# Longer DMA rows, products on one engine, and a dealing of tokens in two groups, in a scale-and-duplicate kernel

## The chip, the cores and the metric

The kernel runs on 1 core of one Trainium2 chip. The time is the device time of one execution in microseconds, of which several are taken; the figure for a kernel is the median of its runs. A profile is one execution taken by the hardware profiler. Its span runs from the first to the last instruction of the program; the execution's own time is a little longer.

## The reference

Each of 16 x 1024 = 16384 tokens is a vector of 512 fp32 numbers. It is written out twice (k = 2), each copy multiplied by one weight of its own:

```
batch, seq, hidden = 16, 1024, 512;  k = 2
x_expanded = x[:, :, np.newaxis, :].repeat(k, axis=2)
weights = expert_weights[..., np.newaxis]
return (x_expanded * weights).astype(np.float32)
```

The expert indices are an input and are not used. The program reads 2 KB per token and writes 4 KB: 33.6 MB in, 67.1 MB out, with 32768 products of a 512-vector and a number, done for 128 tokens at a time.

## The kernel before, in words

The tokens are dealt to the 128 SBUF partitions in equal runs: partition p has tokens 128p to 128p + 127. So in DRAM the input of neighbouring partitions lies 256 KB apart, the output 512 KB. All weights are loaded once into `w_tile` (L44).

The loop takes 8 tokens per partition in each of 16 iterations. `issue_load` (L48) takes an input tile from `x_pool` (three buffers of 16 KB per partition) and fills it with two DMAs of 4 tokens each (L53, L54), both issued from ScalarE's queue; a DMA is 1 MB, one row of 8 KB for each partition. Two tiles are asked for ahead of the loop, and each iteration first asks for the tile two ahead. The DMA instruction stands in ScalarE's program between the products, so it is issued when ScalarE gets there and when the buffer is free.

Each iteration has two halves of 4 tokens. A half takes an output tile from `o_pool` (six buffers of 16 KB per partition), makes 8 products, one for each token and each of the two weights, and stores the tile with one DMA of 2 MB from SyncE's queue (L93), a row of 16 KB for each partition. The eight products of the first half are all on ScalarE (L79). In the second half product 0 is on VectorE and product 4 on GpSimd (L85), six on ScalarE. Nothing else orders the work: a store waits for its products, a product for its load and for a free output tile, a load for the products on the tile that it overwrites. The framework adds these waits from the use of the tiles; it also has a fixed number of DMA semaphores that it hands out in turn, so a DMA may also wait for an older DMA that had the same one.

The lines that matter: L44 weights, L53 and L54 loads, L79 ScalarE products, L85 VectorE and GpSimd products, L93 stores.

Of the kernel before, what the change touches and what calls it, by code (L numbers as in the profile page):

```python
# [1 line left out]

# [4 lines left out]


@with_exitstack
def kernel(  # L10
    ctx: ExitStack,
    tc: tile.TileContext,
    x: bass.AP,
    expert_indices: bass.AP,
    expert_weights: bass.AP,
    out: bass.AP,
):
    nc = tc.nc

    batch, seq, hidden = x.shape  # L20
    k = expert_weights.shape[-1]
    P = nc.NUM_PARTITIONS
    ntok = batch * seq
    assert ntok % P == 0
    A_TOTAL = ntok // P

    xr = x.rearrange("b s h -> (b s) h").rearrange("(p a) h -> p a h", a=A_TOTAL)
    outr = out.rearrange("b s k h -> (b s) (k h)").rearrange(
        "(p a) n -> p a n", a=A_TOTAL
    )  # L30
    wr = expert_weights.rearrange("b s k -> (b s) k").rearrange(
        "(p a) k -> p a k", a=A_TOTAL
    )

    A = 8
    H = A // 2
    n_iters = A_TOTAL // A

    w_pool = ctx.enter_context(tc.tile_pool(name="w_pool", bufs=1))
    x_pool = ctx.enter_context(tc.tile_pool(name="x_pool", bufs=3))  # L40
    o_pool = ctx.enter_context(tc.tile_pool(name="o_pool", bufs=6))

    w_tile = w_pool.tile([P, A_TOTAL, k], mybir.dt.float32)
    nc.sync.dma_start(out=w_tile, in_=wr)  # L44

    x_tiles = {}

    def issue_load(j):  # L48
        if j >= n_iters:
            return  # L50
        t = x_pool.tile([P, A, hidden], mybir.dt.float32)
        a0 = j * A
        nc.scalar.dma_start(out=t[:, 0:H, :], in_=xr[:, a0 : a0 + H, :])  # L53
        nc.scalar.dma_start(out=t[:, H:A, :], in_=xr[:, a0 + H : a0 + A, :])  # L54
        x_tiles[j] = t

    issue_load(0)
    issue_load(1)

    for it in range(n_iters):  # L60
        a0 = it * A
        issue_load(it + 2)
        x_tile = x_tiles.pop(it)

        for half in range(2):
            o_tile = o_pool.tile([P, H, k, hidden], mybir.dt.float32)
            base = half * H
            opc = 0
            for ai in range(base, base + H):
                for kk in range(k):  # L70
                    w_ap = w_tile[:, a0 + ai, kk : kk + 1]
                    eng = nc.scalar
                    if half == 1:
                        if opc == 0 or opc == 8:
                            eng = nc.vector
                        elif opc == 4:
                            eng = nc.gpsimd
                    if eng is nc.scalar:
                        nc.scalar.mul(  # L79
                            out=o_tile[:, ai - base, kk, :],  # L80
                            in_=x_tile[:, ai, :],
                            mul=w_ap,
                        )
                    else:
                        eng.tensor_scalar(  # L85
                            out=o_tile[:, ai - base, kk, :],
                            in0=x_tile[:, ai, :],
                            scalar1=w_ap,
                            scalar2=None,
                            op0=mybir.AluOpType.mult,  # L90
                        )
                    opc += 1
            nc.sync.dma_start(  # L93
                out=outr[:, a0 + base : a0 + base + H, :], in_=o_tile
            )


# [1 line left out]
_INS = ['x', 'expert_indices', 'expert_weights']  # L99
_OUTS = [((16, 1024, 2, 512), 'float32')]  # L100


# [23 lines left out]
```

## Time and profile before

| | us |
|---|---|
| median of 4 runs | 243.84 |
| lowest and highest | 242.65 and 247.66 |
| the profiled execution, its own time | 243.26 |
| its span | 241.2 |
| ScalarE busy | 140.2 |
| GpSimd busy | 29.7 |
| VectorE busy | 7.9 |

The page says that 100.82 MB were moved, a mean of 418 GB/s over the span, in 9363 DMA packets; 1040 of them are under 512 bytes (semaphore updates, 16 for each of 65 DMAs). Issues of DMAs by kind, with the count, the KB of each and the median time in us from issue to landing:

```profile
out_dram<-o_tile SPq DMA_DIRECT2D x32, 2048.0 KB, 25.3
t<-in_x_dram ACTq DMA_DIRECT2D x32, 1024.0 KB, 28.1
w_tile<-in_expert_weights_dram SPq DMA_DIRECT2D x1, 128.0 KB, 4.6
```

How to read the lines: a product group names the line, the engine, the operation, the tile written and the tiles read, the shape and the count; after the bar stand the busy time in us and the mean of one in ns, after the second bar the time for which the engine sat idle before these instructions and what ended that. DVE is VectorE, ACT is ScalarE, POOL is GpSimd, SPq and ACTq are the sequencers of SyncE and ScalarE as they issue DMAs. A row of the timeline has the start, the time it took, and what ran. In the picture of 40 slices a digit is the busy share of a slice in tenths, 9 being 90% or more.

### The profile page before, as it was taken

The numbers are of one execution on the slowest core, as the hardware profiler recorded it, in microseconds if no ns is written. First come the engines' busy times: TensorE is split into PE (matmuls) and PEld (weight loads), VectorE is DVE, ScalarE is ACT, GpSimd is POOL, SyncE is SP. The second block draws the span as 40 slices with busy tenths as digits, with TensorE's granted clock in tenths as the row PEclk, the third lists the DMA queues.
The fourth block names the chain that finished last, engine by engine and source line by source line (L and its number), as shares of the span: only waits on it lengthen the run. The fifth ranks groups of instructions, "written<-read, shape, count | busy, mean of one in ns | idle before, by whom it ended". The sixth has DMA issues, their size and how long they took to land.

```text
span 241.2 us, 500 instructions
## 1 busy us (share of the span) xinstructions
DVE 7.9 (3%) x16; ACT 140.2 (58%) x225; POOL 29.7 (12%) x20
## 2 busy tenths in 40 slices
DVE  0000000000000000000000000000000000000000
ACT  1989874909458192773918549095590996563000
POOL 0330303002030110302002030020301103020000
DMA  7999999999999999999999999999999999999994
GB/s 254 427 368 429 424 429 444 421 429 423 428 440 418 439 418 436 432 425 435 421 435 431 427 437 420 433 431 425 442 420 433 429 432 435 420 439 431 424 435 201
DMA packets 9363, 100.82 MB, mean 418 GB/s; under 512 B 1040, under 2 KB 1168, under 8 KB 1168
## 3 DMA queue, kind: packets, MB, share of 16 engines
q1 hardware_dynamic: 4752, 67.24, 65.2%
q10 hardware_dynamic: 4608, 33.56, 33.5%
q14 instruction: 3, 0.02, 0.0%
HBM read 33.69 MB, written 67.11 MB: 418 GB/s over the span
## 4 chain that ended last, share of the span: by engine, by line
DMA 83%; ACT 3%; ACTq 0%; issue 0%
DMA t<-in_x_dram 83%; ACT o_tile L79 3%; ACTq L121 0%; ACTq L79 0%
## 5 line engine op out<-in xcount | busy, mean ns | idle before, releaser
L79 ACT ACTIVATE o_tile<-t,w_tile 128x512 f32<-128x512 f32 x224 | 138.9, 706 | 73.5 <-DMA t<-in_x_dram 71.9
L85 POOL TENSOR_SCALAR o_tile<-t,w_tile 128x512 f32<-128x512 f32 x16 | 29.5, 1842 | 187.4 <-DMA t<-in_x_dram 187.4
L85 DVE TENSOR_SCALAR o_tile<-t,w_tile 128x512 f32<-128x512 f32 x16 | 7.9, 492 | 208.0 <-DMA t<-in_x_dram 208.0
L79 ACT ACT_TABLE_LOAD x1 | 1.3, 1283 | 5.4 <-DMA w_tile<-in_expert_weights_dram 5.4
L110 POOL MEMSET const-float32-0.0<- 128x1 f32 x1 | 0.1, 98 | 0.2 <-issue 0.2
L110 POOL MEMSET const-bfloat16-1.0<- 128x1 bf16 x1 | 0.1, 102 | 0.0
L110 POOL MEMSET const-uint8-127<- 128x1 uint8 x1 | 0.1, 101 | 0.0
L110 POOL MEMSET const-float32-1.0<- 128x1 f32 x1 | 0.1, 98 | 0.0
## 6 DMA issues: line engine op xcount, KB each, us to landing
out_dram<-o_tile SPq DMA_DIRECT2D x32, 2048.0 KB, 25.3
t<-in_x_dram ACTq DMA_DIRECT2D x32, 1024.0 KB, 28.1
w_tile<-in_expert_weights_dram SPq DMA_DIRECT2D x1, 128.0 KB, 4.6
```

Of the source, the lines that this page charges most:

```text
L79: nc.scalar.mul(out=o_tile[:, ai - base, kk, :], in_=x_tile[:, ai, :], mul=w_ap,)
L85: eng.tensor_scalar(out=o_tile[:, ai - base, kk, :], in0=x_tile[:, ai, :], scalar1=w_ap, scalar2=None, op0=mybir.AluOpType.mult,)
L110: nc = _bacc.Bacc("TRN2", target_bir_lowering=False, num_devices=1)
```

## The change

- Tokens are dealt in two groups. The first 65 x 128 tokens are dealt in runs of 65 to each partition, the other 63 x 128 in runs of 63. In DRAM the rows of neighbouring partitions lie 130 KB (input) and 260 KB (output) apart in the first group, 126 and 252 KB in the second.
- Loads are larger: five of 13 tokens in the first group, then 16, 16, 16 and 15 in the second, one DMA for each tile, rows of 26 to 32 KB per partition. There are two input buffers of 32 KB per partition (before: three of 16 KB).
- Stores are of 8 tokens, and of the 5 or 7 that are left over at the end of an input tile: rows of 32, 20 or 28 KB. There are four output buffers of 32 KB per partition (before: six of 16 KB).
- All 256 products are on VectorE. ScalarE's queue only issues loads, SyncE's queue only the two weight loads (one for each group) and the stores. No load is asked for ahead of the loop by hand: the first two go out at once, since there are two free tiles, and each later one when its tile is free.

The core of the diff, old lines with a minus, new ones with a plus:

```
-    A = 8
-    H = A // 2
-    n_iters = A_TOTAL // A
+    TX = 16
+    TO = 8
+    groups = [[[13], [13], [13], [13], [13]], [[16], [16], [16], [15]]]
...
-    x_pool = ctx.enter_context(tc.tile_pool(name="x_pool", bufs=3))
-    o_pool = ctx.enter_context(tc.tile_pool(name="o_pool", bufs=6))
+    x_pool = ctx.enter_context(tc.tile_pool(name="x_pool", bufs=2))
+    o_pool = ctx.enter_context(tc.tile_pool(name="o_pool", bufs=4))
...
+    def rows(of_all, done, T):
+        return of_all[done * P : (done + T) * P, :].rearrange(
+            "(p a) n -> p (a n)", a=T
+        )
...
+    for group in groups:
+        T = sum(sum(t) for t in group)
+        xr = rows(xf, done, T)
+        outr = rows(of, done, T)
+        a0 = 0
+        for pieces in group:
+            x_tile = x_pool.tile([P, TX * hidden], f32)
+            at = 0
+            for n in pieces:
+                nc.scalar.dma_start(
+                    out=x_tile[:, at * hidden : (at + n) * hidden],
+                    in_=xr[:, (a0 + at) * hidden : (a0 + at + n) * hidden],
+                )
+                at += n
+            ends = [sum(pieces[: i + 1]) for i in range(len(pieces))]
+            first = 0
+            for t in range(at):
+                if t % TO == 0:
+                    o_tile = o_pool.tile([P, TO * row], f32)
                 for kk in range(k):
...
-                    eng = nc.scalar
-                    if half == 1:
-                        if opc == 0 or opc == 8:
-                            eng = nc.vector
-                        elif opc == 4:
-                            eng = nc.gpsimd
...
+                    nc.vector.tensor_scalar(
+                        out=o_tile[:, o : o + hidden],
+                        in0=x_tile[:, t * hidden : (t + 1) * hidden],
+                        scalar1=w_tile[:, c : c + 1],
+                        scalar2=None,
+                        op0=mybir.AluOpType.mult,
+                    )
+                if t + 1 in ends or (t + 1) % TO == 0:
+                    nc.sync.dma_start(
+                        out=outr[:, (a0 + first) * row : (a0 + t + 1) * row],
+                        in_=o_tile[:, first % TO * row : (t % TO + 1) * row],
+                    )
+                    first = t + 1
+            a0 += at
+        done += T
```

More of the change, by code (lines that the diff above doesn't have):

```diff
@@ L25 @@
     A_TOTAL = ntok // P
[L27 to L33, printed above, removed]
-    A = 8
-    H = A // 2
-    n_iters = A_TOTAL // A
-    w_pool = ctx.enter_context(tc.tile_pool(name="w_pool", bufs=1))
-    x_pool = ctx.enter_context(tc.tile_pool(name="x_pool", bufs=3))
@@ L41 @@
-    o_pool = ctx.enter_context(tc.tile_pool(name="o_pool", bufs=6))
[L43 to L69, printed above, removed]
-                for kk in range(k):
-                    w_ap = w_tile[:, a0 + ai, kk : kk + 1]
-                    eng = nc.scalar
-                    if half == 1:
-                        if opc == 0 or opc == 8:
-                            eng = nc.vector
-                        elif opc == 4:
-                            eng = nc.gpsimd
[L78 to L95, printed above, removed]
@@ new lines @@
+    f32 = mybir.dt.float32
+    row = k * hidden
+    TX = 16
+    TO = 8
+    groups = [[[13], [13], [13], [13], [13]], [[16], [16], [16], [15]]]
+    assert sum(sum(sum(t) for t in g) for g in groups) == A_TOTAL
+    xf = x.rearrange("b s h -> (b s) h")
+    of = out.rearrange("b s k h -> (b s) (k h)")
+    wf = expert_weights.rearrange("b s k -> (b s) k")
+    w_pool = ctx.enter_context(tc.tile_pool(name="w_pool", bufs=1))
+    x_pool = ctx.enter_context(tc.tile_pool(name="x_pool", bufs=2))
@@ new lines @@
+    o_pool = ctx.enter_context(tc.tile_pool(name="o_pool", bufs=4))
+    w_tile = w_pool.tile([P, A_TOTAL * k], f32)
+    def rows(of_all, done, T):
+        return of_all[done * P : (done + T) * P, :].rearrange(
+            "(p a) n -> p (a n)", a=T
+        )
+    done = 0
+    for group in groups:
+        T = sum(sum(t) for t in group)
+        nc.sync.dma_start(
+            out=w_tile[:, done * k : (done + T) * k], in_=rows(wf, done, T)
+        )
+        done += T
+    done = 0
+    for group in groups:
+        T = sum(sum(t) for t in group)
+        xr = rows(xf, done, T)
[15 more added lines that the diff above has]
+                    o_tile = o_pool.tile([P, TO * row], f32)
+                for kk in range(k):
+                    c = (done + a0 + t) * k + kk
+                    o = t % TO * row + kk * hidden
+                    nc.vector.tensor_scalar(
[6 more added lines that the diff above has]
+                if t + 1 in ends or (t + 1) % TO == 0:
+                    nc.sync.dma_start(
+                        out=outr[:, (a0 + first) * row : (a0 + t + 1) * row],
+                        in_=o_tile[:, first % TO * row : (t % TO + 1) * row],
+                    )
+                    first = t + 1
+            a0 += at
+        done += T
```

## The prediction

> **What bounds the kernel now.** I read the 40 slices and the DMA queues on the page first, because one row there is full from end to end:
>
> ```profile
> DMA  7999999999999999999999999999999999999994
> ...
> q1 hardware_dynamic: 4752, 67.24, 65.2%
> q10 hardware_dynamic: 4608, 33.56, 33.5%
> ```
>
> The two queues (q1: stores and the weights, q10: loads) fill 65.2 + 33.5 = 98.7% of the sixteen DMA engines' span. ScalarE, the busiest compute engine, is at 58%. So the question is what the change does to the bytes per us of the DMA engines and to the stretches where they lack work. The next view is the table of stretches: span, then busy us of VectorE, ScalarE and GpSimd, the clock, the DMA share and GB/s.
>
> ```profile
> 0.00:4.00 4.00, 0.00 (x0) 0.00 (x0) 0.19 (x4) 1.00 0.53 163
> 5.00:13.00 8.00, 0.49 (x1) 7.61 (x12) 1.84 (x1) 1.00 1.01 428
> 14.00:17.00 3.00, 0.00 (x0) 2.37 (x5) 1.32 (x1) 1.00 0.98 289
> 17.00:19.00 2.00, 0.00 (x0) 2.00 (x4) 0.00 (x0) 1.00 1.07 459
> 18.00:218.00 200.00, 6.90 (x14) 127.14 (x206) 25.78 (x14) 1.00 1.01 430
> 220.00:236.00 16.00, 0.00 (x0) 0.00 (x0) 0.00 (x0) 1.00 1.01 432
> 237.00:241.20 4.20, 0.00 (x0) 0.00 (x0) 0.00 (x0) 1.00 0.24 101
> ```
>
> Loads alone (5 to 13 us) move 428 GB/s, stores alone (220 to 236) 432, both together 430. The span splits accordingly: 100.82 MB at 430 GB/s is 234.5 us; the remaining 6.7 us are 2.5 lost in the first 4 us (0.65 MB, 1.5 us' worth), 0.85 lost between 14 and 19 us (1.79 MB in 5 us), and 3.2 lost after 237 us. Nothing else can be won or lost but these.
>
> Third, the groups, for the duration of each kind of product, and the timeline of ScalarE, whose 15 in a row show the distance from one start to the next:
>
> ```profile
> L79 ACT ACTIVATE o_tile<-t,w_tile 128x512 f32<-128x512 f32 x224 | 138.9, 706 | 73.5 <-DMA t<-in_x_dram 71.9
> L85 POOL TENSOR_SCALAR o_tile<-t,w_tile 128x512 f32<-128x512 f32 x16 | 29.5, 1842 | 187.4 <-DMA t<-in_x_dram 187.4
> L85 DVE TENSOR_SCALAR o_tile<-t,w_tile 128x512 f32<-128x512 f32 x16 | 7.9, 492 | 208.0 <-DMA t<-in_x_dram 208.0
> ```
>
> ```profile
> 0.71 0.40 ACTq L53 DMA_DIRECT2D t<-in_x_dram  x1
> ...
> 6.67 9.29 ACT L79 ACTIVATE o_tile<-t,w_tile 128x512 f32<-128x512 f32 x15
> 8.51 0.49 DVE L85 TENSOR_SCALAR o_tile<-t,w_tile 128x512 f32<-128x512 f32 x1 [8.51 <-DMA t<-in_x_dram]
> 8.58 1.84 POOL L85 TENSOR_SCALAR o_tile<-t,w_tile 128x512 f32<-128x512 f32 x1 [8.16 <-DMA t<-in_x_dram]
> 11.71 32.60 SPq L93 DMA_DIRECT2D out_dram<-o_tile  x7
> ```
>
> VectorE's first product starts at 8.51, when tile 0's second half has landed; the first store is issued at 11.71.
>
> **Part 1: longer rows.** A DMA moves one row per partition, so 8 rows per DMA engine. Before, an engine moves 32 x 8 = 256 load rows of 8 KB and 256 store rows of 16 KB; after, 9 x 8 = 72 load rows of 26 to 32 KB and 18 x 8 = 144 store rows of 20 to 32 KB. The bytes are the same. The rates above price a row: 8192 x 16 / 428 GB/s = 306.2 ns for a load row, 16384 x 16 / 432 GB/s = 606.8 ns for a store row; 8 KB more cost 300.6, so 5.6 ns are fixed per row. The trace's packet records say the same (309 and 611 ns at the median, so 302 per 8 KB and 7 fixed). There are 512 - 216 = 296 rows fewer per engine: 296 x 5.6 = **-1.7 us**; ends 0 (the fit does not carry to 32 KB) and -2.1 (7 ns). By the fit a 32 KB row takes 1.208 us, a 26 KB row 0.983, a 20 KB row 0.757.
>
> **Part 2: row pitch (65 and 63 tokens).** The distance between partitions' rows in DRAM goes from 256 and 512 KB to 126 to 260 KB, no power of two. In the packet records store rows take 611 ns at the 5th, 50th and 95th percentile, load rows 309: none waits for a place in memory. I take 0; the price if this is wrong is in the rivals. The Trainium skill ("DMA: Bandwidth & Descriptors", Latency and other measured facts) gives 207 GB/s per direction at a pitch of 512 KiB against 214 once padded, on copies between DRAM tensors, and advises padding. By that ratio the stream here would gain about 3%, an estimate of 7 us; the equal rates of 428 at one pitch and 432 at twice that pitch speak against it.
>
> **Part 3: products to VectorE.** Removed: 224 ScalarE products, its table load, 16 GpSimd products. Added: 240 on VectorE. Its 16 products of before all came after a wait, at 0.49 us each. On ScalarE one takes 0.706 us, but 15 stand in 9.29 us: (9.29 - 0.71) / 14 = 0.61 from start to start, 0.87 of a duration. I take 0.87 x 0.49 = 0.42 us on VectorE, ends 0.39 (0.49 less ScalarE's 0.09) and 0.49. All 256 then take 108 us (125 at most) against some 232 of DMA: hidden in the middle, on the path only at the start. The skill ("VectorE: DVE Perf Modes", the errata section) gives 58 cycles + 512/2 at 0.96 GHz, an estimate of 0.33 us, by which the gap of part 4 would be zero; no row here shows it.
>
> **Part 4: the start.** The first load grows from 1 to 3.4 MB, and only two loads (6.8 MB) can be issued before products free a tile; before it was 6.3 MB in six. Tile 0 of before is 16 rows x 0.306 = 4.9 us and was usable at 8.51, so 3.6 us are start and landing. After: 3.6 + 8 x 0.983 = 11.5, and 11.6 with the second weight DMA (8 short rows per engine). Load 1 ends 7.9 later, less about 0.5 for landing: the loads run dry at **19.0**. Store 0 needs 16 products: 11.6 + 16 x 0.42 = 18.3 (17.8 to 19.4). From issue to first row: the first load, with nothing queued ahead, was issued at 0.71 and its first row stands at 1.92 in the packet records, 1.2 us; the first store, with over 1 MB of loads ahead, was issued at 11.71 and its first row stands at 15.84, 4.1 us. After the change next to nothing is queued ahead, so I take 1.3 and keep 4.1 as the other end. First store row 19.6: DMA idles **+0.6 us**; ends 0 and 4.5 (19.4 + 4.1 - 19.0).
>
> Past that the engines stay fed. Store 1 and load 2 are issued at 18.3 + 10 x 0.42 = 22.5, while store 0 (8 x 1.208 = 9.7 us) runs; store 0, load 2 and store 1 hold 9.7 + 7.9 + 6.1 = 23.7 us of work, to 43; store 2 joins at 29, store 3 and load 3 at 33, another 23.7. In the steady state a token costs VectorE 0.84 us and the DMA engines 128 x 6 KB at 434 GB/s, 1.81 us; while VectorE fills one output tile (6.7 us) up to three others (29 us of rows) are queued. This cover also holds at the end, so the tail stays; if it failed, each store would add its products' 6.7 us.
>
> **Part 5: queues and waits.** ScalarE's queue now holds loads alone, so none stands behind products; each from the third on waits for the last product on its tile, and in the built order some also for an older store to be complete. Behind it are only later loads. On SyncE 18 stores stand behind each other, each waiting for its own products; a late one delays only stores that VectorE makes later anyway. Cost 0, hidden by the same backlog.
>
> **Two unpriced terms.** The 0.85 us dip at 14 to 19 us, where the load rows just ahead of the first stores took about 530 ns instead of 309, may vanish (loads are over by then) or repeat: 0 to -0.85; I take 0. The sixteen engines finished between 237.7 and 239.8 us; with rows twice as long the last may end one old row later, 0 to +0.6; I take 0.
>
> **Sum**, against the profiled execution: 241.2 - 1.7 + 0.6 = 240.1 us of span. That execution took 243.26 us, 2.06 outside the span: 242.2. The median of the runs shown, 243.84, is 0.6 above it, so I forecast **242.7**. Own range: -2.1 and -0.85 without a gap, 240.9; no row saving, a gap of 0.6 and +0.6, 245.0.
>
> **Rivals.** (A) Slower: the first store comes late. Place: DMA idle from 19.0. It decides once the first store row stands after 19.0 + 1.7 = 20.7 us. With 4.1 us from issue to row it is 22.4, a gap of 3.4: 243.84 - 1.7 + 3.4 = 245.5; with 0.49 us per product also, gap 4.5, 246.6. For it: the only store that the trace shows starting. Against it: the queue ahead is empty here.
> (B) Faster by pitch: the equal rates hide a loss common to loads and stores. The best slice of before ran at 444 GB/s; all bytes at that take 227.1 us, 7.4 less: 236.4, and 237.0 with the gap. Against it: constant row times.
> (C) The good ends together: dip gone, gap nil, 2.1 saved: 240.9.
> (D) Rows of 32 KB run slower per byte than the fit, say by the 1% between 428 and 432: 2.3 us lost in place of 1.7 won, with the gap 243.84 + 2.9 = 246.7. No row of this length is in the trace.
>
> **Numbers.** Forecast 0.62, A 0.15, B 0.06, C 0.12, D 0.05. The range of 240.6 to 245.3 holds the forecast, C and the milder half of A, and leaves out B, D and the rest of A. One per cent, about what a measurement of this kernel can tell, is 241.4 and 246.3. Faster by more: B, most of C and a little of the forecast, 0.22; slower by more: A's worse half, most of D and a remainder for long rows, 0.11; within, 0.67.
>
> **What would show it.** Row price: stretches between 30 and 210 us at 433 to 435 GB/s (B: 440 or more; D: under 430). Products: 0.42 us from start to start. Start: first product at 11.6, first store issued at 18.3, one gap before 21 us (A: DMA empty until 22 or more). No gap later; a second one would break the argument on backlog, and a tail longer than 4 us that on the end.

## The result and the profile after

The median of 12 runs is 247.2 us (243.85 to 249.27), against 242.94 us for the kernel before (17 runs). Of the executions within 1.5% of the fastest of their kernel the ratio is 1.0119, with a 95% interval of 1.0077 to 1.016: slower by 1.2%, where 0.5% faster was forecast and 245.3 was the upper end. The profiled execution took 245.34 us, its span is 243.6, so 2.4 us more than before, where 1.1 less had been worked out. It is the third shortest of the twelve: the trace accounts for its 2.4 us, not for all of the 4.3 us by which the two medians differ.

The page of the kernel after: engines in 40 slices, bytes per slice, the two queues, and the shares of the chain that ended last.

```profile
DVE  0199920880283345150905490551804594600000
...
DMA  7999999999999999999999999999999999999981
GB/s 289 428 424 425 386 387 425 405 463 404 433 432 466 414 419 425 459 436 392 420 440 438 405 428 424 437 432 418 415 432 447 447 431 452 436 436 431 408 384 85
...
q1 hardware_dynamic: 2880, 67.24, 65.0%
q10 hardware_dynamic: 1296, 33.56, 32.5%
...
DMA 71%; DVE 15%; issue 0%; DVEq 0%
```

The DMA row is still full nearly to the end, and the packets are 4178 in place of 9363: the change did what it says. But the bytes per slice are uneven (386, 387, 405 and 392 in places), and the last two slices fall off earlier than before. The shares of q1 and q10 also show that a full DMA row does not mean that the engines do well: they sum to 97.5%, at 414 GB/s.

The stretches, with the same columns as before but without ScalarE, which has no products now:

```profile
0.00:4.00 4.00, 0.00 (x0) 0.20 (x4) 1.00 0.66 223
5.00:13.00 8.00, 1.59 (x5) 0.00 (x0) 1.00 1.01 431
18.00:30.00 12.00, 12.00 (x31) 0.00 (x0) 1.00 0.99 381
30.00:210.00 180.00, 83.26 (x209) 0.00 (x0) 1.00 1.00 429
220.00:236.00 16.00, 0.00 (x0) 0.00 (x0) 1.00 1.01 434
236.00:240.00 4.00, 0.00 (x0) 0.00 (x0) 1.00 0.47 201
240.00:243.60 3.60, 0.00 (x0) 0.00 (x0) 1.00 0.09 40
```

Stores alone at the end reach 434 GB/s, as the price of a long row says. Two stretches are bad: 18 to 30 us, where a DMA share of 0.99 moves 381 GB/s, so the engines were busy but slow; and everything after 236 us, where 201 and 40 GB/s at shares of 0.47 and 0.09 mean that most engines had finished and a few went on.

The timeline of the start:

```profile
11.41 20.67 DVE L83 TENSOR_SCALAR o_tile<-x_tile,w_tile 128x512 f32<-128x512 f32 x52 [11.41 <-DMA x_tile<-in_x_dram]
17.86 14.58 SPq L91 DMA_DIRECT2D out_dram<-o_tile  x4
43.76 6.42 DVE L83 TENSOR_SCALAR o_tile<-x_tile,w_tile 128x512 f32<-128x512 f32 x16 [11.68 <-DMA x_tile<-in_x_dram]
```

First product at 11.41 (11.6 forecast), first store issued at 17.86 (18.3 forecast), its first row in the packet records at 18.71. Sixteen products in 6.42 us with a last one of 0.48 are 0.396 us from start to start (0.42 forecast).

The group of products and the issues of DMAs, from the page:

```profile
L83 DVE TENSOR_SCALAR o_tile<-x_tile,w_tile 128x512 f32<-128x512 f32 x256 | 102.6, 480 | 108.1 <-DMA out_dram<-o_tile 81.8
...
out_dram<-o_tile SPq DMA_DIRECT2D x12, 4096.0 KB, 41.2
x_tile<-in_x_dram ACTq DMA_DIRECT2D x5, 3328.0 KB, 21.5
```

All products take 102.6 us and VectorE idles for 108.1, of which 81.8 until a store has emptied an output tile. A store lands 41.2 us after its issue, although its own rows take 8 x 1.2 = 9.7: some 30 us of rows are queued ahead of it, so the engines were not short of work.

Two readings of the trace's records carry the rest. The packet records give each row's time. A row is called slow here if it took over 20 ns more than its length usually takes, and the excess of all of them is divided by sixteen engines. The landing records give, for each DMA, the time at which each of its sixteen engines was done; the spread is the last less the first. For some stores, spread by time of first landing:

```
before, store first landing at  37.8   67.1   96.4  125.6  154.9  184.1  213.4  238.0
        spread, us               1.7    2.1    2.1    2.1    2.2    2.4    1.9    2.2
after,  store first landing at  32.7   64.5   85.2  110.6  136.2  177.0  209.6  237.4
        spread, us               0.2    0.9    3.0    5.2    3.7    8.6    5.2    5.2
```

After the change, eleven engines finish the last store within 0.3 us of each other, and five are 3.8 to 5.2 us later. In the middle of a run a large spread need not cost anything: e6 below, which is faster than the kernel before, has stores with 4.6 and 5.3 us (147 and 176 us) and ends with 2.8. So the experiments are compared by the last store. With the packet records the two spans add up, in us per engine (the last two lines count the time in which fewer than sixteen rows were under way):

| | before | after | difference |
|---|---|---|---|
| rows and semaphore packets at their usual times | 236.6 | 233.9 | -2.7 |
| more than sixteen rows under way at once (rows overlap) | -2.0 | -0.9 | +1.1 |
| excess of slow rows | 1.6 | 3.4 | +1.8 |
| engines without a row, first 20 us | 2.0 | 2.1 | 0 |
| engines without a row, last 20 us | 2.9 | 5.0 | +2.0 |

But for rounding, the differences sum to the 2.4 us by which the spans differ. The fixed cost of rows was saved nearly as forecast (2.68 less 1.14, so 1.5 of 1.7 us); it was lost more than twice over in slow rows and in five late engines.

### The profile page after: what moved, and what is told of

The parts are those of the page before. It is cut to its first block, busy times and chain, and to the rows that moved or that the text cites. A ratio compares the mean times of both kernels' runs of the same rounds, so it can differ in the third digit from the quotient of the medians.

```text
span 243.6 us, 368 instructions
## 1 busy us (share of the span) xinstructions
DVE 102.6 (42%) x256; POOL 0.2 (0%) x4
## 2 busy tenths in 40 slices
DMA packets 4178, 100.81 MB, mean 414 GB/s; under 512 B 592, under 2 KB 720, under 8 KB 720
## 4 chain that ended last, share of the span: by engine, by line
DMA 71%; DVE 15%; issue 0%; DVEq 0%
DMA out_dram<-o_tile 57%; DVE o_tile L83 15%; DMA x_tile<-in_x_dram 13%; DVEq L123 0%; DVEq L83 0%
## 5 line engine op out<-in xcount | busy, mean ns | idle before, releaser
L83 DVE TENSOR_SCALAR o_tile<-x_tile,w_tile 128x512 f32<-128x512 f32 x256 | 102.6, 480 | 108.1 <-DMA out_dram<-o_tile 81.8
## 6 DMA issues: line engine op xcount, KB each, us to landing
out_dram<-o_tile SPq DMA_DIRECT2D x12, 4096.0 KB, 41.2
```

Source lines behind the costliest of these rows:

```text
L83: nc.vector.tensor_scalar(out=o_tile[:, o : o + hidden], in0=x_tile[:, t * hidden : (t + 1) * hidden], scalar1=w_tile[:, c : c + 1], scala ...
```

## The experiments

The ratio is always to the kernel before in runs on the same chip. The spread is that of the last store, the slow rows are those that start after 45 us (before: 2.2 us and 0.17 us per engine; after: 5.2 and 1.4). Spread and slow rows are those of one execution, which for e7, e8, e9, e10, e15 and e17 is the shortest of its runs. On the chip of e1 to e4 the kernel before itself varied from 242.57 to 246.47 us (median 245.35, elsewhere 242.7 to 242.9), so these four ratios have wide intervals and come out low: the medians of e1 to e4 are 243.2, 243.0, 250.2 and 244.8 us.

| | load / store rows, KB | dealt | ratio (95%) | spread | slow rows |
|---|---|---|---|---|---|
| e1 | 32 / 32 | 128 | 0.995 (0.990 to 1.000) | 3.2 | 1.2 |
| e2 | 8 / 16 | 72, 56 | 0.995 (0.990 to 1.001) | 1.6 | 0.04 |
| e3 | 16 / 32 | 72, 56 | 1.022 (1.015 to 1.029) | 10.0 | 3.5 |
| e4 | 8 / 16 | 128 | 1.000 (0.994 to 1.006) | 1.9 | 1.2 |
| e5 | 16 / 32 | 128 | 1.027 (1.024 to 1.031) | 8.8 | 3.0 |
| e6 | 32 / 32 | 64, 64 | 0.994 (0.992 to 0.996) | 2.8 | 0.1 |
| e7 | 26 to 32 / 16 | 65, 63 | 1.006 (1.004 to 1.008) | 2.0 | 0.9 |
| e8 | 26 / 32 and 20 | 128 | 1.020 (1.018 to 1.021) | 5.8 | 1.7 |
| e9 | 26 / 28 and 24 | 65, 63 | 1.011 (1.010 to 1.013) | 5.6 | 0.5 |
| e10 | 16 / 32 | 128 | 1.027 (1.025 to 1.028) | 8.0 | 2.5 |
| e11 | 16 / 16 | 128 | 0.996 (0.995 to 0.998) | 1.5 | 0.05 |
| e12 | as changed | 65, 63 | 1.014 (1.010 to 1.019) | 4.2 | 1.4 |
| e13 | 26 / 26 | 65, 63 | 1.000 (0.998 to 1.001) | 3.2 | 1.7 |
| e14 | 32 / 16 | 128 | 1.001 (1.000 to 1.002) | 1.1 | 2.9 |
| e15 | 12 / 24 | 128 | 1.006 (1.004 to 1.008) | 2.2 | 1.4 |
| e16 | 12 to 16 / 16 | 65, 63 | 1.002 (1.000 to 1.004) | 1.4 | 0.1 |
| e17 | as changed, one queue | 65, 63 | 1.011 (1.007 to 1.015) | 3.6 | 0.9 |
| e18 | 32 / 32, one queue | 64, 64 | 1.005 (1.002 to 1.007) | 4.4 | 1.3 |

### First four: dealing, a dry queue, VectorE

e1 is the kernel after with the tokens dealt as before:

```
-    groups = [[[13], [13], [13], [13], [13]], [[16], [16], [16], [15]]]
+    groups = [[[16]] * 8]
```

> The changed kernel with the tokens dealt as before, in one run of 128 tokens per partition (rows 256 KB apart in the input, 512 KB in the output), and eight input tiles of 16 tokens; all else as changed. In the changed kernel the sixteen DMA engines finish the last store 5.2 us apart, against 2.2 before, and row records far above their usual time stand some 4 us after loads are issued to an empty load queue. Theory dry (a load queue that has run dry and fills again slows the rows under way, and some engines more than others): the tile sizes are kept, so the spread at the end stays at 4 us or more and the time at 244 to 248 us. Theory pitch (rows that are no power of two apart meet in memory): spread back to about 2 us, few slow rows, 240 to 242.5 us.

e2 is the kernel before, dealt in two groups; `dealt` picks the group that token a0 belongs to:

```
+    G = (72, 56)
+    def dealt(t, a0, n):
+        first, T = (0, G[0]) if a0 < G[0] else (G[0], G[1])
+        v = t[first * P : (first + T) * P, :].rearrange("(p a) n -> p a n", a=T)
+        return v[:, a0 - first : a0 - first + n, :]
...
-        nc.scalar.dma_start(out=t[:, 0:H, :], in_=xr[:, a0 : a0 + H, :])
+        nc.scalar.dma_start(out=t[:, 0:H, :], in_=dealt(xf, a0, H))
```

> The kernel before with nothing changed but the dealing: two groups of 72 and 56 tokens per partition (both whole numbers of its 8-token tiles), so rows lie 144 and 288 KB, then 112 and 224 KB apart. Theory dry: row sizes and queues are as before, so 242 to 243.5 us and a spread of about 2 us at the end. Theory pitch: slow rows appear in the middle, 244.5 us or more.

e3 is the kernel after with short loads:

```
-    TX = 16
+    TX = 8
-    groups = [[[13], [13], [13], [13], [13]], [[16], [16], [16], [15]]]
+    groups = [[[8]] * 9, [[8]] * 7]
-    x_pool = ctx.enter_context(tc.tile_pool(name="x_pool", bufs=2))
+    x_pool = ctx.enter_context(tc.tile_pool(name="x_pool", bufs=4))
```

> The changed kernel with input tiles of 8 tokens in four buffers (the same 64 KB) in place of 13 to 16 tokens in two, dealt 72 and 56; stores of 8 tokens, 32 KB rows, VectorE alone. A load row is then half a store row, as before, and an input tile comes free after 6.4 us of products, so the load queue should seldom be empty. Theory dry: spread at the end 2.5 us or less, no slow rows after 40 us, 240 to 242.5 us. Theory pitch, and also theory long stores (32 KB store rows are the cause): slow rows stay, 244 us or more.

e4 is the kernel before with `eng = nc.vector` for every product.

> The kernel before with all 256 products on VectorE, loads and stores as they were. VectorE needs 0.4 us from start to start in the changed kernel, ScalarE 0.61, so the first store goes out a little earlier. Theories dry and pitch: 242 to 243.5 us, no slow rows in the middle. Theory products (VectorE's accesses slow the DMA rows): slow rows and 244 us or more.

The dealing at short rows changes nothing that the interval can tell (e2), which theory pitch had missed. e1 was about as fast as the kernel before, which pointed to the dealing, though its 243.2 us, its spread of 3.2 and its slow rows (1.2) lie outside what either theory had said. But e3 was the slowest of these four, though its loads were always queued: theory dry falls with it, and with e1, whose loads do run dry. e4 decides little: its interval holds no change, but its 244.8 us and 1.2 us of slow rows are also what theory products had asked for. What speaks against the products as a cause are e6 and e11 below, which have all of them on VectorE, next to no slow rows after 45 us, and less time than the kernel before. What was left was a mixture: long rows at a dealing that is no power of two.

### Second four: the dealing against the shape of the pieces

e5 is e3 with `groups = [[[8]] * 16]`.

> e3 with its one difference to e1 in dealing undone: input tiles of 8 tokens in four buffers, stores of 8 tokens, but all tokens dealt in one run of 128 per partition (rows 256 and 512 KB apart). e3 took 1.022 of the kernel before and its last store ended 10 us apart between engines; theory dry is refuted by that, since its load queue was never empty. Theory meet (32 KB store rows whose starts are no power of two apart run slow on some engines): 0.99 to 1.005 of the kernel before, spread at the end under 3.5 us, hardly a slow store row after 45 us. Theory shape (long stores beside short loads are the cause, whatever the dealing): 1.015 or more and a spread of 7 us or more.

e6 is the kernel after with `groups = [[[16]] * 4, [[16]] * 4]`.

> The changed kernel dealt in two groups of 64 and 64 tokens, tiles of 16: rows 128 KB apart in the input and 256 KB in the output, a power of two again, though half the distance of before and in two groups. Theory meet: 0.99 to 1.003 of the kernel before, spread under 3.5 us. Theory distance (it is the shorter distance, or the two groups, that cost): 1.01 or more, as the changed kernel.

e7 is the kernel after with `TO = 4` and eight output buffers.

> The changed kernel, dealt 65 and 63 with loads of 13 to 16 tokens as changed, but with output tiles of 4 tokens in eight buffers: store rows of 16 KB (4 KB for the fifth-wheel token of each input tile of 13, 12 KB at the end). Theory meet: slow store rows go, 0.99 to 1.005 of the kernel before, spread under 3 us. Theory dealing alone (65 and 63 cost whatever the store rows): 1.01 or more.

e8 is the kernel after with `groups = [[[13]] * 9 + [[11]]]`.

> The changed kernel's uneven pieces without its dealing: one run of 128 tokens per partition in nine tiles of 13 and one of 11, so stores of 8, 5 and at last 3 tokens that start at offsets of 52 KB. Theory meet: 0.99 to 1.005 of the kernel before. Theory pieces (5-token stores and loads of 26 KB cost): 1.01 or more.

e5 and e8 are dealt as before and are slow, so theory meet falls: the dealing is not needed for the loss. What is left is the shape of the pieces. e7, at 1.006, lies just outside what theory meet had allowed, and well below the change. The bytes per slice of e6 and then of e5, from their pages:

```profile
GB/s 273 444 441 421 437 367 432 432 437 437 437 437 432 437 437 426 437 437 437 415 437 437 421 404 437 433 437 437 437 437 437 437 437 437 437 437 437 437 432 109
```

```profile
GB/s 272 434 375 402 453 426 439 428 402 436 418 434 436 399 447 402 452 383 378 418 428 423 471 402 415 435 426 441 420 428 431 455 434 436 423 423 434 428 249 32
```

e6 has 437 in most slices and one clean edge at the end: this is the steady stream that the row price had promised. e5, with loads half as long, swings between 375 and 471, and its 39th slice is down to 249 because most engines are done.

### Third four: equal rows

e9 is the kernel after with stores in halves of a tile:

```
-            ends = [sum(pieces[: i + 1]) for i in range(len(pieces))]
+            ends = [(at + 1) // 2, at]
-                if t % TO == 0:
+                if t == first:
...
-                if t + 1 in ends or (t + 1) % TO == 0:
+                if t + 1 in ends:
...
```

> The changed kernel, dealt 65 and 63 in the same nine loads, but each input tile stored in two halves as equal as they go: 7 and 6 tokens of 13 (rows of 28 and 24 KB beside load rows of 26), 8 and 8 of 16, 8 and 7 of 15. The same number of DMAs and the same bytes. e1 and e6 (32 KB loads, 32 KB stores) were fast at either dealing, e8 (26 KB loads, 32 and 20 KB stores) slow without the dealing. Theory uneven (long load and store rows of unequal length, taken in turn by the engines, let some engines fall behind): 0.99 to 1.004 of the kernel before, spread at the end under 3.5 us. Theory odd (any row that is not a whole 8, 16 or 32 KB, or not at such an address, costs): 1.008 or more.

e10 is e1 with `groups = [[[8, 8]] * 8]`, and stores of 8 tokens kept by `ends = [at]`.

> e1 (one run of 128, two input tiles of 16 tokens, 32 KB store rows) with each load cut into two DMAs of 8 tokens, so load rows of 16 KB beside store rows of 32 KB; tiles, products and stores as in e1, and the load queue runs dry as in e1. Theory uneven: 1.01 or more and a spread of 5 us or more, as e5. Theory tiles (e5 is slow because its four small input tiles keep the load queue always full): 0.99 to 1.003, as e1.

e11 is e5 with `TO = 4` and eight output buffers.

> e5 with its store rows halved: load tiles of 8 tokens in four buffers (16 KB rows), stores of 4 tokens from eight buffers (16 KB rows), one run of 128. Theory uneven: load and store rows are equal, so 0.99 to 1.004 and a spread under 3 us, against 1.027 for e5. Theory tiles (small input tiles that keep the load queue full): 1.015 or more.

e12 is the kernel after, unedited.

> The changed kernel once more, beside the others. All theories: 1.008 to 1.016 of the kernel before; the engines' spread at the end again 4 us or more, a handful of them late. If the spread in this profile is small while the time is high, the spread does not carry the loss.

Two pairs that differ in one row length point the same way. e1 against e10: halving the load rows, in the same tiles, moves the ratio from 0.995 to 1.027 (243.2 to 249.3 us). e5 against e11: halving the store rows as well moves it from 1.027 to 0.996. Both pairs differ in one thing more. In e10 the load queue did not run dry as was expected: the longest time without a load row between the first load and the last is 1.5 us, in e1 14.3; in e5 it is 1.2, in e11 7.2. A load queue that is never empty is not enough for a loss, since in the kernel before and in e2 no such time is over 1 us; but beside long stores it stays a rival for the 2.7%, which no run separates. For the change itself e13 below does. e9 missed the forecast of theory uneven: rows within 8% of each other were no better than the change. It has one engine 5.6 us behind, the others are within 2.2.

### Fourth four: exactly equal, and how far the rule goes

e13 is the kernel after with two stores for each tile, each of as many products as the tile has tokens:

```
+            for half in range(2):
+                o_tile = o_pool.tile([P, TO * row], f32)
+                for i in range(at):
+                    t, kk = divmod(half * at + i, k)
...
+                o = a0 * row + half * at * hidden
+                nc.sync.dma_start(
+                    out=outr[:, o : o + at * hidden], in_=o_tile[:, : at * hidden]
+                )
```

> The changed kernel, dealt 65 and 63 in the same nine loads, with every store exactly as long as its load: two stores for each input tile of 13 products (6.5 tokens, 26 KB), then 16 and 15 products (32 and 30 KB). 18 stores as changed, same bytes. e9, with 28 and 24 KB beside 26, stayed at 1.011. Theory equal (engines stay together only while load and store rows are equal; any inequality of long rows lets some fall behind): 0.99 to 1.003 of the kernel before, spread at the end under 3.3 us. Theory odd (rows of 26 KB cost whatever stands beside them): 1.008 or more, spread 4 us or more.

e14 is e1 with `TO = 4` and eight output buffers.

> e1 (one run of 128, loads of 16 tokens) with output tiles of 4 tokens in eight buffers: load rows of 32 KB, store rows of 16 KB, the ratio of e5 turned round. e7, much the same at 65 and 63, stood at 1.006. Theory equal: slower than e1's 0.995 by half a per cent or more, 1.0 to 1.03. Theory long stores (unequal rows cost only where the store row is the longer and above 16 KB): 0.99 to 0.999.

e15 is the kernel after with `groups = [[[6]] * 21 + [[2]]]`, `TX = 6`, `TO = 6` and five buffers of each kind.

> One run of 128, loads of 6 tokens (12 KB rows, five buffers) and stores of 6 (24 KB rows, five buffers), 21 tiles of 6 and one of 2: the ratio 1 to 2 of the kernel before (8 and 16 KB, 1.0) and of e5 (16 and 32 KB, 1.027), half way between. Theory equal with a cost that grows with the rows: between them, 1.003 to 1.02. Theory threshold at 32 KB stores: 0.99 to 1.002.

e16 is the kernel after with `groups = [[[7, 6]] * 5, [[8, 8]] * 3 + [[8, 7]]]`, `TO = 4`, eight output buffers and `ends = [at]`.

> The changed kernel, dealt 65 and 63, same input tiles, with rows cut on both sides: each load in two DMAs (7 and 6 tokens, then 8 and 8, rows of 12 to 16 KB), stores of 4 tokens from eight buffers (16 KB, 4 KB for the thirteenth token, 12 KB at the end). Theory equal: unequal only a little and rows short, so what the engines lose on each other is small: 0.99 to 1.004. Theory odd or dealing: 1.008 or more.

e13 keeps the dealing, the loads and the number of stores of the changed kernel and makes the rows equal: 1.012 becomes 1.000, with an interval that ends below every interval of the change. It also settles theory odd, since rows of 26 KB are all it has in the first group. Its load queue runs dry as that of the change does (longest time without a load row 11.9 us, in the change 12.2). Its spread is 3.2 us. Its slow rows cost as much as in the change (1.7 against 1.4), but no few engines stay far behind the rest: the middle of the sixteen finishes at 238.4 us and the last at 240.3, in the two profiles of the change at 237.6 and 242.6, and at 238.4 and 242.0 (e12). The end of the stretches of e13, then of e9:

```profile
236.00:238.00 2.00, 0.00 (x0) 0.00 (x0) 1.00 0.61 261
238.00:240.00 2.00, 0.00 (x0) 0.00 (x0) 1.00 0.18 77
240.00:242.00 2.00, 0.00 (x0) 0.00 (x0) 1.00 0.00 0
```

```profile
236.00:238.00 2.00, 0.00 (x0) 0.00 (x0) 1.00 0.30 129
238.00:240.00 2.00, 0.00 (x0) 0.00 (x0) 1.00 0.03 14
240.00:242.00 2.00, 0.00 (x0) 0.00 (x0) 1.00 0.07 29
```

e9's engines are done earlier on the whole (129 against 261 GB/s after 236 us), and yet e9 ends later: a share of 0.07 of sixteen engines is the one that is late. At a ratio of 1 to 2 the cost grows with the rows: 8 and 16 KB 1.0, 12 and 24 KB 1.006, 16 and 32 KB 1.027. With store rows of 16 KB unequal loads cost little (e7, e14, e16: 1.001 to 1.006); e14 lies at the very edge between its two theories. So the direction may matter: every run that lost more than 1% has store rows over 16 KB of which some are longer than the load rows beside them. No run has stores over 16 KB that are all shorter than the loads. That e13 stays half a per cent behind e6 is not explained, and neither is that e9, with rows so nearly equal, loses as much as the change.

### Last two: one queue

e17 is the kernel after with the loads issued from SyncE, two ahead:

```
+    def load(j):
+        if j < len(tiles):
+            done, T, a0, at = tiles[j]
+            x_tiles[j] = x_pool.tile([P, TX * hidden], f32, name="x_tile")
+            nc.sync.dma_start(
+                out=x_tiles[j][:, : at * hidden],
+                in_=rows(xf, done, T)[:, a0 * hidden : (a0 + at) * hidden],
+            )
+    load(0)
+    load(1)
+    for j, (done, T, a0, at) in enumerate(tiles):
...
+        load(j + 2)
```

> The changed kernel with its own tiles and dealing (65 and 63, loads of 13 to 16 tokens, stores of 8 and 5), but the loads issued from SyncE too: two ahead, then each load behind the two stores of the tile whose buffer it takes. With one queue every DMA engine moves its rows in one and the same order, and none chooses between a load row and a store row. Theory turns (engines fall behind because each takes unequal rows in turn from two queues): hardly a slow row past the start, spread at the end under 2 us, 0.985 to 1.0 of the kernel before, unless the queue runs empty while a load waits behind stores, which would show as a gap in the DMA row. Theory rows (unequal long rows are slow in themselves): 1.008 or more, spread 4 us or more.

e18 is e17 with `groups = [[[16]] * 4, [[16]] * 4]`.

> e17 dealt 64 and 64 with tiles of 16, as e6, which is the fastest so far (0.994, spread 2.8 us). Theory turns: as e17, 0.985 to 0.996, spread under 2 us. Theory rows: as e6, 0.992 to 0.997.

Theory turns falls. With one queue there are no turns between two, and still engines fall behind, with equal rows too. Theory rows missed e18 as well (1.005 where 0.997 was its upper end). The queue did not run empty: between 20 us and the last 20 us fewer than sixteen rows were under way for 0.05 us (e17) and 0.04 us (e18) in all, but the first 20 us have 2.7 and 2.5 us of this, against 2.1 in the change and 2.0 in e6. In e18 the landing records show the spread grow from load to load: 0.8 us at the second, 1.3, 2.3, 3.2, 3.4, 4.1 and 4.4 at the last. There, all engines pass from a run of store rows to a run of load rows; that some lose more by it than others would fit, but no run shows it apart. In e6, with the same rows from two queues, the last load lands within 0.6 us, and the slow rows after 45 us sum to 0.1 us.

## Why the prediction was wrong

**The bound** was read rightly: DMA engines from end to end. "Nothing else can be won or lost but these" was not: slow rows after 45 us, for which the sum had no term, cost 1.2 us more than before.

**Part 1, longer rows**: the mechanism was right, -1.7 forecast, -1.5 measured (2.68 less the 1.14 by which overlapping rows saved more before). e6 and e11, where hardly a row is slow after 45 us, are 0.6 and 0.4% faster than the kernel before.

**Part 2, row pitch**, taken at 0: e2 gives no loss or gain that its interval can tell. e1 (256 and 512 KB apart) and e6 (128 and 256 KB) have nearly the same ratio, but 243.2 and 241.0 us, on different chips, so a part of some 0.9% for the pitch is neither shown nor excluded. Rival B's 444 GB/s never came: the mean between 30 and 210 us is 429. The Trainium skill ("DMA: Bandwidth & Descriptors", Latency and other measured facts) gives 207 GB/s for DRAM-to-DRAM copies at a pitch of 512 KiB, and its 214 belongs to a pitch of 4 MiB padded by 4 KiB. These rows between SBUF and DRAM take the same 309, 611 or 1213 ns at the median at every pitch tried.

**Part 3, products**: 0.396 us where 0.42 was taken; the skill's table would have had 0.33 ("VectorE: DVE Perf Modes", the errata section). The measurement lies between, and nothing hung on it.

**Part 4, the start**: every time within 0.9 us, and no gap where +0.6 was forecast: engines without a row in the first 20 us are 2.1 us against 2.0. Rival A, a late first store, is refuted: 0.85 us from issue to first row.

**The step that failed** is "Two unpriced terms". The prediction let the dip "vanish ... or repeat: 0 to -0.85; I take 0", and had the last engine end "one old row later, 0 to +0.6; I take 0". The dip repeated and was deeper (slow rows between 12 and 45 us: 0.96 us before, 1.6 after), and slow rows went on after 45 us (0.17 before, 1.4 after): +1.8 us in all. The reason given for the dip to vanish, that the loads are over by then, held only until they came back: no load row starts from 19.0 to 26.8 us, and 0.9 of the 1.6 us lie between 24 and 27. Later, 1.2 of the 1.4 us lie at 108 to 116 and 140 to 155 us, around the return of the loads at 111.0 and 140.6 after 10 and 12 us without a row. The spread went from 2.2 to 5.2 us, and the engines without a row at the end cost +2.0. With the rows' -1.5 that makes +2.3. The sentence on part 4 that "the tail stays" rested on queued work. The work was there, but a queue that is full does not help an engine that is behind: at the end of the last store eleven engines were done within 0.3 us, and their standing free did not spare the other five their 3.8 to 5.2 us. The prediction's own sign for this, a tail longer than 4 us, came.

**Rival D** came nearest in size (rows of 32 KB slower than the fit, +2.9), and its sign came too (under 430 GB/s between 30 and 210 us; 429 was measured), but by luck: e6 and e1 have nothing but rows of 32 KB and run near the fitted price (1213 ns at the median, 1208 by the fit). It is the change's lengths beside each other (26 with 32 and 20) that cost, as e13 shows. Why unequal long rows slow some engines, and which ones, stays open: turns between two queues are not needed (e17), nor a dry load queue (e3), which is not enough either (e6 has up to 14.5 us without a load row), or the dealing (e8). VectorE alone does not do it (e6, e11), but every run with long rows has its products there, so that it plays no part is not shown.

## What to carry to other kernels

When the DMA engines are the bound, longer rows save a small fixed cost each, but a transfer is done when its slowest engine is: look at how far apart the engines land, first and last, not at the mean share alone. If loads and stores are both long, make their rows the same length, or at least do not let the stores be the longer ones; here 32 and 32 KB (e6, 0.994) or 16 and 16 KB (e11, 0.996) beat both kernels, while 16 beside 32 KB lost 2.7%. The unequal pieces that came with the uneven dealing were what cost here: dealt 64 and 64 in tiles of 16, the same code stands at 0.994 of the kernel before, dealt 65 and 63 at 1.012.

## What the runs showed of the hardware that was not expected

- A row's time is nearly constant: 309 ns for 8 KB, 611 for 16 KB and 1213 for 32 KB at the median, so 7 ns fixed and about 302 for each 8 KB, at any of the dealings tried. Slow rows are a separate event: after 45 us of the changed kernel half of them took 1.1 to 1.4 times the usual time, and none over twice (2427 ns for 32 KB; the longest of any run is 2755 ns, in e1).
- When a second stream joins one that runs, the rows under way slow down: 49 of the 57 load rows that start between 14 and 16 us in the kernel before are slow, and the median of the 57 is 542 ns in place of 309, and slow rows between 12 and 45 us cost 0.8 to 1.6 us per engine in every kernel with two queues. With one queue it was 2.0 us (e17) and 0.5 (e18).
- A load queue and a store queue are served about row by row: between 17 and 30 us of the kernel before 17.5 load rows and 17.6 store rows start per us, in every single us between 11 and 22 of each, and a load and a store land side by side (74.21 and 74.38 us, 81.56 and 81.72). The rows' lengths therefore set how the bytes are shared while both queues have work.
- Loads and stores from one queue in long runs were slower than from two (e18 1.005, e6 0.994), at the same rows.
